# A block of ones at the front of a hybrid decoder layer, earlier raw weights, probabilities scaled on ScalarE, and accumulators split as they are finished

## The chip, the cores and the metric

The kernel runs on one core of a Trainium2 chip. The metric is the device time of one execution in microseconds (us). Five engines work side by side, each in the order of its own list of instructions, and wait for each other by semaphores: TensorE (PE, with its weight loads as PEld), VectorE (DVE), ScalarE (ACT), GpSimd (POOL) and SyncE (SP), which here only starts transfers.

## The reference

One layer on x of 2048 tokens by 1024 channels, float32, with 256 memory tokens. The lines that matter here:

```python
h = rms_norm(x, norm_g)                       # one combined projection w_in of h
a = rwkv7_mix(...)                            # 8 heads x 64
b = sliding_window_sink_attn(...)             # 8 heads x 64, window 128
kv = rms_norm(mem, mem_norm_g) @ w_mem_kv     # memory_cross_attn: keys and values of mem
p = softmax(q @ km.T * 128 ** -0.5); c = p @ vm   # 4 heads x 128
...
# each branch * SiLU(gate) is projected to 1024 channels, weighted by sigmoid gates,
# the three are added, and the sum goes through w_out and is added to x
```

## The kernel before, in words

Tokens are worked in four superblocks of 512 (`sb` 0 to 3). Activations stand transposed, channels on partitions. Every large product is in float32 precision by three matmuls: both operands are split in a high part (rounded to the matmul format, by ScalarE) and a low part (the rest, by VectorE), and `gemm3` (L426) issues high by high (L430), low by high and high by low (L431, L432). A weight block goes through `wblock` (L405): a DMA of 128x512 into a `raw` buffer (three of them, L411), the high copy on ScalarE (L412), the subtraction on VectorE (L413), both into a `whl` buffer (eight). In superblock 0 the finished pair is written to DRAM (L416), and superblocks 1 to 3 fetch it from there whole (L408), without ScalarE or VectorE. So superblock 0 has much more work on those two engines than the others.

At the front, `mem` and the first x blocks are loaded (L341, L351) on the SP queue, then the constants, then raw weights. `norm_T` (L435) squares the rows (L446 on ScalarE, L444 on VectorE), scales them (L451), transposes them on TensorE (L456, 128x128 pieces) and copies the transposed columns out of PSUM as high part (L460, ScalarE) and low part (L461, VectorE); for `mem` these columns are the tiles `mB`. `mem_kv` then multiplies them with `w_mem_kv` (L430 to L432 with 256 columns). `onesw`, a block of ones, is made at L476 to L479 and is used later for column sums.

Then superblock 0 weaves two streams: the recurrent branch (`stream_r`; its projections, the token statistics L472 and the products L731 of its inverse, whose operands QE, QO and BK come from a VectorE chain L703 to L719) and the attention branches (`stream_f`: `cross_head` with the probability scaling L961, the window attention with its exponentials L1066, SiLU gates L898/L899, two merges, the gates L1104). At its end comes the third merge, branch a with `merge(0, ...)` (L1119 multiplies, L1120 adds onto the accumulator, a tile `mB`; eight of them, o = 0 to 7). `x_cols` (L1182, L1184, L1185) prepares the next superblock's x. `output` (L1122) splits all eight accumulators (L1126 on ScalarE into a `g` buffer, L1128 on VectorE into an `mB` buffer), multiplies them with `w_out` (L1137 to L1139) and adds x (L1144).

The order in which each engine holds its instructions isn't the program's. `order` (L265 and on) lets a list scheduler, `lay_out`, deal all instructions to the engines while the program is built, by a modelled time for each and, among those ready, by the lowest `rank`. A rank is the program's position, with corrections in `steps` (L133): the writes of `whl` tiles get 1000 less, but not below a floor of 15, and readers of PSUM outside TensorE get 600 less. On the chip, each engine then runs its list strictly in that order.

## Time and profile before

| | |
|---|---|
| runs | 2280.58, 2281.17, 2286.04 us; median 2281.17 |
| profiled execution | 2283.99 us, its span 2282.2 us, mean granted TensorE clock 0.995 |
| TensorE busy | 2241.2 us (98%), 13684 matmuls |
| VectorE, ScalarE, GpSimd busy | 1541.3 us (68%), 916.9 us (40%), 148.6 us (7%) |
| TensorE busy from 600 to 1100 us (superblocks 1 and 2 in part) | 498.16 of 500 us |
| TensorE busy from 300 to 320 us, 560 to 582 us, 582 to 590 us | 14.20 of 20, 20.50 of 22, 3.81 of 8 us |
| VectorE busy in the same three stretches | 18.10, 20.05, 7.25 us |

The profiled execution is the one from which all rows are taken; its time is the span and 1.8 us around it. A row of the waits names the engine and line that waited, the engine, tile and line that it waited for last, the sum of time, the number of times and the longest. A row of the timeline gives the start, the duration, engine, line and operation, the tiles written and read, and in brackets the idle time before it and what ended it. A row of the windows gives, for a stretch of time, the busy time of PE, PEld, DVE, ACT and POOL with the number of instructions, the granted TensorE clock (1.00 is full speed), the share of the DMA engines in use and GB/s. Superblock 0 ends, by its last output product, at 628.5 us.

### The profile page before, as it was taken

To read this page: it belongs to the slowest core of one execution; us is meant where nothing else is said; L and a number is where in the kernel's file an instruction comes from. 1 tells how busy PE (TensorE), PEld (TensorE's weight loads), DVE (VectorE), ACT (ScalarE), POOL (GpSimd) and SP (SyncE) were. 2 spreads that over 40 slices of the span, in tenths; PEclk is the share of its full clock that TensorE was granted. 3 is DMA by queue.
4 is the path that set the end of the run, shared out by engine and by line. 5 is a ranking of instruction groups with operands and counts; after the bars stand their busy time and mean duration, and the time that the engine had idled before them with its cause. 6 is when DMAs were issued, how large, how long until landed. Compare 5 with 4: busy or idle time off the path is not lost.

```text
span 2282.2 us, 36933 instructions
## 1 busy us (share of the span) xinstructions
PE 2241.2 (98%) x13684; PEld 1814.2 (79%) x13684; DVE 1541.3 (68%) x3967; ACT 916.9 (40%) x2006; POOL 148.6 (7%) x209
## 2 busy tenths in 40 slices
PE   7999989999999999999999999999999999999999
PEld 6788778777788877878888877877888887777887
DVE  6799689775568777954427967884345795796312
ACT  5554564545244354433214344442222535434210
POOL 2000010000000010000001001000000001000000
PEclk9999999999999999999999999999999999999999
DMA  6767546679844443437774434445675444343655
GB/s 215 273 225 252 185 153 217 222 258 341 302 155 160 146 148 130 157 138 239 232 265 129 151 127 139 157 136 183 231 252 196 155 147 151 115 153 121 204 193 193
DMA packets 146226, 430.55 MB, mean 189 GB/s; under 512 B 16640, under 2 KB 21120, under 8 KB 146048
## 3 DMA queue, kind: packets, MB, share of 16 engines
q1 hardware_dynamic: 129920, 398.83, 52.1%
q10 hardware_dynamic: 16128, 29.37, 3.9%
q8 instruction: 109, 1.79, 0.3%
q14 instruction: 69, 0.57, 0.1%
HBM read 333.24 MB, written 94.90 MB: 188 GB/s over the span
## 4 chain that ended last, share of the span: by engine, by line
PE 70%; DVE 12%; ACT 3%; DMA 2%; issue 1%; POOL 0%; SPq 0%; ACTq 0%; DVEq 0%; POOLq 0%
PE mm L431 17%; PE mm L430 17%; PE mm L432 16%; PE rw L731 1%; DVE ibc L779 1%; PE mm L1139 1%; PE mm L1137 1%; PE mm L1138 1%; PE rw L852 1%; PE oo L1092 1%; DVE ibc L780 1%; PE oo L967 1%; PE rw L845 1%; DVE Yi L781 1%; PE rw L837 1%
## 5 line engine op out<-in xcount | busy, mean ns | idle before, releaser
L430 PE MATMUL mm<-hH,whl 128*128 128x512 f32 x1888 | 751.1, 398 | 4.6 <-DVE g L899 3.8
L431 PE MATMUL mm<-hL,whl 128*128 128x512 f32 x1888 | 752.4, 398 | 0.0
L432 PE MATMUL mm<-hH,whl 128*128 128x512 f32 x1888 | 747.4, 396 | 0.0
L430 PEld LDWEIGHTS mm<-hH,whl 128*128 128x128 f32 x1888 | 355.7, 188 | 76.7 <-DVE g L899 4.3
L431 PEld LDWEIGHTS mm<-hL,whl 128*128 128x128 f32 x1888 | 355.6, 188 | 71.1 <-issue 0.7
L432 PEld LDWEIGHTS mm<-hH,whl 128*128 128x128 f32 x1888 | 355.8, 188 | 68.6
L412 ACT ACTIVATE whl<-raw 128x512 fp32r<-128x512 f32 x178 | 111.7, 630 | 183.4 <-PE mm L432 79.6
L413 DVE TENSOR_TENSOR whl<-raw,whl 128x512 fp32r<-128x512 f32 x178 | 123.6, 696 | 65.7 <-ACT whl L412 64.6
L430 PE MATMUL mm<-yh,whl 128*128 128x512 f32 x384 | 152.8, 398 | 1.4 <-DVE g L1119 1.4
L431 PE MATMUL mm<-yl,whl 128*128 128x512 f32 x384 | 151.4, 394 | 0.0
L432 PE MATMUL mm<-yh,whl 128*128 128x512 f32 x384 | 151.3, 394 | 0.0
L843 ACT ACTIVATE SP<-Z,Pl 64x64 f32<-64x64 f32 x256 | 88.3, 345 | 118.7 <-DVE Z L853 114.9
L779 DVE STREAM_SHUFFLE ibc<-Nc 128x496 f32<-128x496 f32 (+30 forms) x248 | 113.2, 474 | 0.1
L1119 DVE SCALAR_TENSOR_TENSOR g<-g,mm 128x512 f32<-128x512 f32 x32 | 21.9, 686 | 127.5 <-PE mm L432 127.4
L780 DVE TENSOR_TENSOR ibc<-ibc,Yi 128x496 f32<-128x496 f32 (+30 forms) x248 | 104.7, 422 | 3.5
L781 DVE TENSOR_TENSOR Yi<-Yi,ibc 128x496 f32<-128x496 f32 (+30 forms) x248 | 103.6, 418 | 1.2
L853 DVE SCALAR_TENSOR_TENSOR Z<-rw,Pl,SP 64x64 f32<-64x64 f32 x224 | 63.5, 283 | 46.6 <-PE rw L852 42.9
L1104 ACT ACTIVATE gt<-mm 128x512 f32<-128x512 f32 x64 | 37.8, 591 | 129.3 <-PE mm L432 129.2
L430 PEld LDWEIGHTS mm<-yh,whl 128*128 128x128 f32 x384 | 72.1, 188 | 16.6 <-DVE g L1119 2.5
L432 PEld LDWEIGHTS mm<-yh,whl 128*128 128x128 f32 x384 | 72.1, 188 | 14.8
L1066 ACT ACTIVATE g<-g,mxs,st 128x256 f32<-128x256 f32 (+1 forms) x128 | 74.6, 584 | 22.8 <-DVE mxs L1059 22.5
L431 PEld LDWEIGHTS mm<-yl,whl 128*128 128x128 f32 x384 | 72.2, 188 | 13.9
(1882 smaller groups left out, 3789.6 us busy)
## 6 DMA issues: line engine op xcount, KB each, us to landing
whl<-k SPq DMA_DIRECT2D x486, 512.0 KB, 3.3
k<-whl SPq DMA_DIRECT2D x162, 512.0 KB, 3.2
raw<-in_w_in SPq DMA_DIRECT2D x118, 256.0 KB, 3.7
g<-in_x ACTq DMA_DIRECT2D x32, 256.0 KB, 5.0
out<-g ACTq DMA_DIRECT2D x32, 256.0 KB, 3.6
raw<-in_w_proj SPq DMA_DIRECT2D x24, 256.0 KB, 3.6
rt<-in_x ACTq DMA_DIRECT2D x24, 256.0 KB, 5.2
rt<-in_xt ACTq DMA_DIRECT2D x24, 256.0 KB, 5.5
```

Of the source, the lines that this page charges most:

```text
L412: S.activation(w[:, 0], raw, AF.Copy)
L413: V.tensor_tensor(w[:, 1], raw, w[:, 0].bitcast(F32), op=ALU.subtract)
L430: PE.matmul(out, lh, rh, start=i == 0, stop=False)
L431: PE.matmul(out, lh, rl, start=False, stop=False)
L432: PE.matmul(out, ll, rh, start=False, stop=i == n - 1)
L779: V.stream_shuffle(bc[:, :, :w], N_[:, :, s + 1:], [s] * 32)
L780: V.tensor_tensor(bc[:, :, :w], bc[:, :, :w], Y[:, :, s:s + 1].to_broadcast([128, n, w]), op=ALU.mult)
L781: V.tensor_tensor(Y[:, :, s + 1:], Y[:, :, s + 1:], bc[:, :, :w], op=ALU.add)
L843: S.activation(SP[h, i], Z[h, i, e, c], AF.Copy, scale=g[4][h, c:c + 1])
L853: upds = [V.scalar_tensor_tensor(Sst[h, g[0]] if c == NC_ - 1 else Z[h, i, e, c + 1], pS[h, i, e], g[4][h, c:c + 1], SP[h, i], op0=ALU.mul ...
L1066: S.activation(prs[b][:, i, m0:], prs[b][:, i, m0:], AF.Exp, scale=r2[:, b, i:i + 1], bias=mx[:, b, i:i + 1], accum_out=mx[:, b, 2 + i:3 + i])
L1104: S.activation(t, gp, AF.Tanh, scale=0.5)
```

## The change

Four edits. (1) The block of ones is made at the very front, and WARM = 22 matmuls of it with itself, 128x512, are issued first of all on TensorE, into a PSUM tile (`idle`) that nobody reads. (2) In `steps`, the DMAs into `raw` tiles get the lowered rank too, and its floor becomes FRONT = 30. (3) `cross_head` scales the probabilities in superblock 0 by ScalarE (16 instructions of 128x256); in the other three by VectorE as before. (4) Each accumulator is split right after its own third merge (`split_acc`), instead of all eight at the start of `output`; `x_cols` follows in the program.

```diff
@@ -23,6 +23,8 @@
 SCRATCH = 1024
 FIRST = 1
 RAW = 3
+WARM = 22
+FRONT = WARM + 8
 C = 64
 NC_ = TB // C
 EPS = 1e-6
@@ -151,8 +153,8 @@
             b.after.append(s)
         byname[ins.name] = s
         s.rank = len(out)
-        if any(r[0].startswith("whl") and (s.bytes or r[5] == F32R) for r in s.writes):
-            s.rank = max(s.rank - ahead, min(s.rank, 15))
+        if any(r[0].startswith(("whl", "raw")) and (s.bytes or r[5] == F32R) for r in s.writes):
+            s.rank = max(s.rank - ahead, min(s.rank, FRONT))
         if s.eng != "PE" and any(r[4] for r in s.reads):
             s.rank -= 600
         if s.eng == "DVE" and s.writes and s.writes[0][0].startswith(("ibc", "Yi")):
@@ -334,6 +336,14 @@
         nc.sync.dma_start(t, A[name] if src is None else src)
         return t
 
+    ones1 = cp.tile([128, 1], F32, name="ones1")
+    V.memset(ones1, 1.0)
+    onesw = bp.tile([128, 128], F32R, name="onesw")
+    S.activation(onesw, ones1.to_broadcast([128, 128]), AF.Copy)
+    idle = o_ps().rearrange("p (a b) -> p a b", a=4)
+    for _ in range(WARM):
+        PE.matmul(idle, onesw, onesw.unsqueeze(1).to_broadcast([128, 4, 128]), start=True, stop=True)
+
     mem0 = []
     for i in range(2):
         mem0.append([g2(), g2()])
@@ -473,10 +483,6 @@
 
     ones2 = bp.tile([128, 128], F32R, name="ones2")
     S.activation(ones2.rearrange("p (a b) -> p a b", a=2), bones.unsqueeze(2).to_broadcast([128, 2, 64]), AF.Copy)
-    ones1 = cp.tile([128, 1], F32, name="ones1")
-    V.memset(ones1, 1.0)
-    onesw = bp.tile([128, 128], F32R, name="onesw")
-    S.activation(onesw, ones1.to_broadcast([128, 128]), AF.Copy)
     eye64 = cp.tile([128, 64], F32, name="eye64")
     V.tensor_tensor(eye64, ident[:, :64], ident[:, 64:], op=ALU.add)
 
@@ -898,6 +904,13 @@
         S.activation(t, o, AF.Tanh, scale=0.5)
         V.scalar_tensor_tensor(t, t, 1.0, o, op0=ALU.add, op1=ALU.mult)
         return t
+
+    def scaled_by(t, c, sb):
+
+        if sb:
+            V.tensor_scalar(t, t, c, None, op0=ALU.mult)
+        else:
+            S.activation(t, t, AF.Copy, scale=c)
 
     def split_y(y, yh, yl, br, j, sb):
         a = yp.tile([128, TB], F32R, name="yh")
@@ -958,7 +971,7 @@
             pt = s_ps().rearrange("p (k i t) -> p k i t", k=2, i=2)
             for i in range(2):
                 q = 2 * t2 + i
-                V.tensor_scalar(prs[t2][:, i], prs[t2][:, i], dn[:, q:q + 1], None, op0=ALU.mult)
+                scaled_by(prs[t2][:, i], dn[:, q:q + 1], sb)
                 for kt in range(2):
                     PE.transpose(pt[:, kt, i], prs[t2][:, i, kt * 128:(kt + 1) * 128], ident)
             pts = g2(shape=(128, 2, 256))
@@ -1119,15 +1132,14 @@
                 V.scalar_tensor_tensor(g, g, 1.0, pp, op0=ALU.add, op1=ALU.mult)
                 V.tensor_tensor(accs[o], accs[o], g, op=ALU.add)
 
-    def output(sb, accs):
-        mh, ml = [], []
-        for o in range(8):
-            a = g2(F32R)
-            S.activation(a, accs[o], AF.Copy)
-            b = mp.tile([128, TB], F32R, name="mB")
-            V.tensor_tensor(b, accs[o], a.bitcast(F32), op=ALU.subtract)
-            mh.append(a)
-            ml.append(b)
+    def split_acc(acc):
+        a = g2(F32R)
+        S.activation(a, acc, AF.Copy)
+        b = mp.tile([128, TB], F32R, name="mB")
+        V.tensor_tensor(b, acc, a.bitcast(F32), op=ALU.subtract)
+        return a, b
+
+    def output(sb, mh, ml):
         for n in range(2):
             op = [mm_ps(), s_ps(), mm_ps(), s_ps()]
             for k in range(8):
@@ -1240,11 +1252,14 @@
         if sb + 1 < nsb:
             rope_tables(sb + 1)
             rb = x_scales(sb + 1)
-        for _ in merge(0, *ya, accs, hT, gates=gates):
-            pass
+        parts = []
+        for o in range(8):
+            for _ in merge(0, *ya, accs, hT, gates=gates, orange=(o,)):
+                pass
+            parts.append(split_acc(accs[o]))
         if rb is not None:
             hT = x_cols(sb + 1, rb)
-        output(sb, accs)
+        output(sb, *zip(*parts))
     order(tc, manual)
     es.close()
```

The line numbers of the changed kernel are other ones: L421 to L423 are L411 to L413 of before, L440 to L442 are L430 to L432, L456 and L454 the squares L446 and L444, L461 the scaling L451, L470 and L471 the copies L460 and L461, L466 the transposes L456, L482 is L472, L737 is L731, L904 is L898, L1079 is L1066, L1132 and L1133 are L1119 and L1120, L1139 is L1128, L1194 and L1197 are L1182 and L1185.

Almost all moves lie in superblock 0; the lists of superblocks 1 to 3 hold the same instructions in practically the same order. Three places:

The front, SP's list. Before, it reads from the first x block on (four `rt` and four `g` tiles are x blocks of 128x512; `c_` tiles are constants):

```order
L351 DMA rt<-in_x 128x512 x4
L351 DMA g_108<-in_x 128x512
L351 DMA g_110<-in_x 128x512
L351 DMA g_112<-in_x 128x512
L351 DMA g_114<-in_x 128x512
L334 DMA c_eye_116<-in_eye 128x32
L334 DMA c_bones<-in_bones 128x2
L334 DMA c_ropec<-in_ropec 128x2
L334 DMA c_sinks<-in_sinks 128x8
L1150 DMA g_340<-in_gmask 128x128
L1150 DMA g_343<-in_amask 128x256
L411 DMA raw<-in_w_mk 128x512 x8
```

Now, from the same place:

```order
L361 DMA rt<-in_x 128x512
L421 DMA raw<-in_w_mk 128x512 x3
L361 DMA rt<-in_x 128x512 x3
L361 DMA g_135<-in_x 128x512
L361 DMA g_137<-in_x 128x512
L361 DMA g_139<-in_x 128x512
L361 DMA g_141<-in_x 128x512
L336 DMA c_eye_143<-in_eye 128x32
L336 DMA c_bones<-in_bones 128x2
L336 DMA c_ropec<-in_ropec 128x2
L336 DMA c_sinks<-in_sinks 128x8
```

Three raw blocks of `w_mk` stand behind the first x block and ahead of the other seven.

ScalarE's list at the front, before, from the second square of `mem` on (the numbers keep the buffers apart; `g2_112` and the `rt` are x):

```order
L446 ACTIVATE ibc_187,ss_181<-g2_92 128x512
L446 ACTIVATE ibc_238,ss_236<-rt_100 128x512
L446 ACTIVATE ibc_242,ss_236<-rt_104 128x512
L446 ACTIVATE ibc_289,ss_236<-g2_108 128x512
L460 ACTIVATE mB_173<-rw_198,c_pv_98 128x256
L446 ACTIVATE ibc_293,ss_236<-g2_112 128x512
L460 ACTIVATE mB_174<-as__207,c_pv_98 128x256
L460 ACTIVATE mB_173<-rw_198,c_pv_98 128x256
L460 ACTIVATE mB_175<-rw_216,c_pv_98 128x256
```

and now:

```order
L456 ACTIVATE ibc_261,ss_259<-rt_127 128x512
L422 ACTIVATE whl_372<-raw_373 128x512
L422 ACTIVATE whl_377<-raw_378 128x512
L422 ACTIVATE whl_411<-raw_412 128x512
L456 ACTIVATE ibc_265,ss_259<-rt_131 128x512
L456 ACTIVATE ibc_312,ss_259<-g2_135 128x512
L470 ACTIVATE mB_196<-rw_221,c_pv_125 128x256
L456 ACTIVATE ibc_316,ss_259<-g2_139 128x512
L470 ACTIVATE mB_197<-as__230,c_pv_125 128x256
L470 ACTIVATE mB_196<-rw_221,c_pv_125 128x256
```

The three high copies of raw weights (L422) stand ahead of the second square of x, and the first copy of transposed `mem` (L470) still stands behind the square of the x block `g2_135`, the second behind that of `g2_139`. VectorE's first subtractions (L423) stand, in the same way, around its scaling of `mem` (L461).

The window attention near 300 us, ScalarE's list. Before (`rt<-rk` belongs to the recurrent branch, `g2_3226` to `g2_3242` hold scores, `g2_3482` is a SiLU gate that leaves PSUM):

```order
L412 ACTIVATE whl_3586<-raw_3587 128x512
L693 ACTIVATE rt_3026<-rk__2966,c_pv_98 128x512
L1066 ACTIVATE g2_3226,mxs_3225<-g2_3226,mxs_3225,st8_3217 128x128 x2
L1066 ACTIVATE g2_3227,mxs_3225<-g2_3227,mxs_3225,st8_3217 128x256 x2
L1066 ACTIVATE g2_3242,mxs_3225<-g2_3242,mxs_3225,st8_3217 128x256
L412 ACTIVATE whl_3644<-raw_3645 128x512
L898 ACTIVATE g2_3482<-mm_3443 128x512
L711 ACTIVATE rt_3047<-rt_2986,dv_126 128x512
```

and now (the scores are `g2_3249` and on, the gate is `g2_3505`):

```order
L422 ACTIVATE whl_3573<-raw_3574 128x512
L717 ACTIVATE rt_3070<-rt_3009,dv_153 128x512
L422 ACTIVATE whl_3609<-raw_3610 128x512
L422 ACTIVATE whl_3667<-raw_3668 128x512
L904 ACTIVATE g2_3505<-mm_3466 128x512
L641 ACTIVATE rk__3443<-mm_3404,dv_153 128x512
L1075 ACTIVATE dns_3346<-dns_3346 128x8
L1079 ACTIVATE g2_3249,mxs_3248<-g2_3249,mxs_3248,st8_3240 128x128 x2
L1079 ACTIVATE g2_3250,mxs_3248<-g2_3250,mxs_3248,st8_3240 128x256
```

The gate's copy out of PSUM stood behind five rows of exponentials, and now stands ahead of them. On TensorE at the same place, four projection matmuls stood between the first and the second group of the products L731 (eight of 128x128 in each), and thirteen stand between the groups of L737 now; and from the statistics (L472, now L482), whose result the products' operands are made from, to the first group it was 22 projection matmuls, and now it is 41.

The end of superblock 0, VectorE's list. Before, from the last third merge's addition on (`hL` and `rt` are the next x, an `mB` of L1128 is a split; the numbers keep the buffers apart):

```order
L1120 TENSOR_TENSOR mB_4476<-mB_4476,g2_5913 128x512
L1185 SCALAR_TENSOR_TENSOR hL_6180<-rt_6201,c_pv_98,hH_6179 128x512
L1182 TENSOR_TENSOR rt_6206<-rt_6206,rt_6001 128x512
L1182 TENSOR_TENSOR rt_6211<-rt_6211,rt_6001 128x512
L413 TENSOR_TENSOR whl_6371<-raw_6372,whl_6371 128x512
L1182 TENSOR_TENSOR rt_6216<-rt_6216,rt_6001 128x512
L1185 SCALAR_TENSOR_TENSOR hL_6180<-rt_6206,c_pv_98,hH_6179 128x512
L1185 SCALAR_TENSOR_TENSOR hL_6180<-rt_6211,c_pv_98,hH_6179 128x512
L413 TENSOR_TENSOR whl_6390<-raw_6391,whl_6390 128x512
L1185 SCALAR_TENSOR_TENSOR hL_6180<-rt_6216,c_pv_98,hH_6179 128x512
L1128 TENSOR_TENSOR mB_6227<-mB_2706,g2_6225 128x512
L413 TENSOR_TENSOR whl_6429<-raw_6430,whl_6429 128x512
```

and now, from the last but one:

```order
L1132 SCALAR_TENSOR_TENSOR g2_5895<-g2_5895,mm_6189 128x512
L1139 TENSOR_TENSOR mB_6180<-mB_3977,g2_6178 128x512
L423 TENSOR_TENSOR whl_6394<-raw_6395,whl_6394 128x512
L1132 SCALAR_TENSOR_TENSOR g2_5936<-g2_5936,mm_6215 128x512
L1133 TENSOR_TENSOR mB_4394<-mB_4394,g2_5895 128x512
L1133 TENSOR_TENSOR mB_4499<-mB_4499,g2_5936 128x512
L423 TENSOR_TENSOR whl_6413<-raw_6414,whl_6413 128x512
L1139 TENSOR_TENSOR mB_6206<-mB_4394,g2_6204 128x512
L1194 TENSOR_TENSOR rt_6246<-rt_6246,rt_6024 128x512
L1139 TENSOR_TENSOR mB_6232<-mB_4499,g2_6230 128x512
L1194 TENSOR_TENSOR rt_6251<-rt_6251,rt_6024 128x512
L423 TENSOR_TENSOR whl_6452<-raw_6453,whl_6452 128x512
```

Before, seven of the eight splits stood behind these seven rows of the next x (L1182, L1185); now six splits stand among the merges, and the last two behind the last addition with one row of the next x between them.

## The prediction

> **What bounds the kernel now.** First the page: TensorE is busy for nearly all of the span. Then the windows, cut where superblock 0 ends, to see where the little idle time lies.
>
> ```profile
> span 2282.2 us, 36933 instructions
> PE 2241.2 (98%) x13684; PEld 1814.2 (79%) x13684; DVE 1541.3 (68%) x3967; ACT 916.9 (40%) x2006; POOL 148.6 (7%) x209
> 0.00:628.50 628.50, 598.16 (x3620) 485.45 (x3621) 480.77 (x1168) 321.12 (x676) 49.43 (x74) 0.98 0.70 240
> 628.50:1180.00 551.50, 548.83 (x3362) 443.75 (x3361) 360.80 (x947) 203.38 (x453) 34.09 (x47) 1.00 0.53 174
> ```
>
> TensorE idles 30.3 us in superblock 0 and 2.7 us in the next one (first column less second), and only in superblock 0 is the clock below full. The change acts there alone, so it can win only these idle times and the slow clock. The waits of TensorE say what the idle time waits for.
>
> ```profile
> PE rw L456 <- DVE g L451: 10.3, 1, 10.3
> PE mm L1139 <- DVE mB L1128: 4.2, 1, 4.2
> PE mm L430 <- DVE g L899: 3.8, 1, 3.8
> PE mm L430 <- ACT whl L412: 3.4, 2, 2.6
> PE mm L430 <- DVE g L1119: 1.4, 1, 1.4
> PE rw L731 <- DVE QO L737: 1.1, 1, 1.1
> PE rw L731 <- DVE whl L737: 1.0, 1, 1.0
> PE as__1483 L472 <- ACT g L921: 0.9, 1, 0.9
> PE rw L731 <- DVE QE L737: 0.9, 1, 0.9
> ```
>
> A wait has a second price. Windows of 3.41 us, laid on the places where the clock changes, show it: columns are the window, TensorE's busy time, and, third from the end, the granted clock.
>
> ```profile
> 135.10:138.51 3.41, 2.51 (x20) 1.91 (x18) 3.32 (x6) 1.11 (x2) 0.00 (x0) 1.00 0.78 272
> 138.51:141.92 3.41, 3.41 (x23) 3.19 (x23) 3.31 (x8) 0.51 (x2) 1.58 (x2) 0.50 0.72 250
> 298.94:302.35 3.41, 1.31 (x9) 0.87 (x8) 3.32 (x8) 3.39 (x13) 0.00 (x0) 1.00 0.97 335
> 302.35:305.77 3.42, 1.68 (x4) 1.41 (x5) 3.30 (x8) 2.52 (x8) 1.54 (x1) 0.50 0.69 246
> 305.77:309.18 3.41, 3.41 (x9) 2.67 (x9) 3.36 (x5) 0.00 (x0) 0.43 (x1) 0.50 0.15 53
> 312.60:316.01 3.41, 1.45 (x8) 0.78 (x7) 3.33 (x6) 0.78 (x2) 0.00 (x0) 1.00 0.40 130
> 316.01:319.42 3.41, 3.41 (x19) 2.79 (x19) 2.96 (x8) 0.62 (x2) 0.00 (x0) 0.50 0.67 219
> 582.25:585.66 3.41, 0.29 (x2) 0.00 (x0) 3.41 (x7) 2.61 (x5) 0.00 (x0) 1.00 0.93 344
> 585.66:589.07 3.41, 2.35 (x6) 1.87 (x7) 3.34 (x6) 0.00 (x0) 0.00 (x0) 0.50 0.83 236
> 589.07:592.49 3.42, 3.42 (x10) 2.64 (x9) 2.47 (x5) 0.63 (x1) 0.00 (x0) 0.50 1.02 405
> 581.92 0.39 PE L1137 MATMUL as__6256<-whl,g 128*128 128x512 f32 x1
> 582.15 0.39 PE L1138 MATMUL as__6256<-whl,g 128*128 128x512 f32 x1
> 588.17 0.63 PE L1139 MATMUL as__6256<-whl,mB 128*128 128x512 f32 x1
> 588.59 0.63 PE L1137 MATMUL mm<-whl,g 128*128 128x512 f32 x1
> ```
>
> After a window with little TensorE work the clock is at half, and stays there until a window was full. The last four rows give the price: starts of 128x512 matmuls lie 0.23 us apart at full clock and 0.42 at half, so 45% of the busy time in a half-clock window is lost. Of the slow windows that is 2.3 us after the wait at 300 (5.09 us of work), 1.5 us after 313, 2.6 us after 582 (5.77 us), and 1.5 us after 135.
>
> **The front.** The rows around the first matmuls (PE's first row ends the wait of 10.3 us):
>
> ```profile
> 2.02 0.31 ACT L479 ACTIVATE onesw<-ones 128x128 fp32r<-128x128 f32 x1
> 10.30 0.47 PE L456 MATMUL rw<-c_ident,g 128*128 128x128 f32 x1 [10.30 <-DVE g L451]
> 10.88 0.63 ACT L446 ACTIVATE ibc<-g 128x512 bf16<-128x512 f32 x1 [1.01 <-DMA g<-in_x]
> 12.09 0.47 ACT L460 ACTIVATE mB<-rw,c_pv 128x256 fp32r<-128x256 f32 x1 [0.48 <-PE rw L456]
> 12.13 1.45 SPq L411 DMA_DIRECT2D raw<-in_w_mk  x3
> 15.94 0.62 ACT L412 ACTIVATE whl<-raw 128x512 fp32r<-128x512 f32 x1
> 16.61 0.58 PE L430 MATMUL mm<-mB,whl 128*128 128x256 f32 x1 [2.64 <-ACT whl L412]
> 17.02 0.68 DVE L413 TENSOR_TENSOR whl<-raw,whl 128x512 fp32r<-128x512 f32 x1
> 19.05:22.46 3.41, 3.41 (x18) 3.41 (x18) 2.54 (x7) 0.63 (x1) 0.99 (x2) 1.00 0.66 214
> 22.46:25.87 3.41, 3.41 (x31) 3.41 (x30) 2.61 (x7) 3.04 (x8) 0.00 (x0) 1.00 0.26 85
> ```
>
> The clock column reads 1.00 here, but 18 matmuls fill the one window and 31 (part of them shorter) the next: TensorE ran at half speed until 22.46, when its first full window had ended.
>
> The warm-up: with `onesw` ready at 2.33, 22 matmuls at 0.42 us would end at 11.6. The first window that they fill ends somewhere between 5.8 and 9.2 us; from then on they go at 0.23, so 8 to 16 are slow and the block ends between 9.0 and 10.6. Until 10.30 TensorE idles, which hides it. At worst it pushes the transposes by 1.3 us.
>
> The raw weights: three 256 KB blocks now pass ahead of seven x blocks on SP's queue. At about 330 GB/s (an estimate from the full windows above) that is 2.4 us later for x. This matters, because ScalarE works in order: its first copy of transposed `mem` (12.09) still stands behind the square of an x block that came at 10.88 and now comes near 13.3, so it starts near 14.1, and the second copy waits for one more x block. VectorE's scaling of `mem` gets two to three subtractions of 0.68 us among its four rows, so the transposes start near 11 instead of 10.30. Against that, the first weights are split long before they are needed, so the first real matmul comes near 14.8 instead of 16.61, and the `mem` columns are complete near 19, some 2 us later than now. Before, the 5.9 us from 16.61 to 22.46 were slow and did 3.2 us worth of work. Now most of that can be done by 19 and the rest by 20.5, if the clock is full: a gain of 2. If the clock has fallen back, the same work ends at 22 to 25.5: from 0 to a loss of 3. If x costs nothing, the gain is 4. **I take 1.5 us of gain**, between the first two, and keep -4 to +3.
>
> A sentence on a rule. The Trainium skill ("TensorE: Matmul & The Clock Gate", Part 4: PE-mode transpose) says that transposes don't count as busy for the clock. By that rule the warm block's clock is lost during the 16 transposes that follow it, the front would gain nothing, and the sum would be 2273.1. The trace doesn't contradict it, and doesn't prove it: the clock stayed at half through the transposes at 10.30 to 14, which filled only about half of their windows. This is the first rival below.
>
> **Near 300 us.** The wait of 3.8 us is for a SiLU gate that holds a PSUM buffer:
>
> ```profile
> 301.82 0.60 ACT L898 ACTIVATE g<-mm 128x512 f32<-128x512 f32 x1
> 304.09 0.80 PE L430 MATMUL mm<-hH,whl 128*128 128x512 f32 x1 [3.84 <-DVE g L899]
> ```
>
> ScalarE came to the gate only at 301.82, behind five rows of exponentials. Now the gate stands ahead of them, so this wait goes, with its 2.3 us of half clock. What is late next is the VectorE chain to the operands of L731: before, 22 matmuls (5.1 us) and this loss of 6.1 us gave it 11 us after the statistics, and 41 matmuls at 0.23, 9.4 us, now stand between. I leave a wait of 2 us, too short for the clock. **Gain 4.1** (0 to 6.1).
>
> At 313 the second group of L731 waited 1.1 and 0.9 us for VectorE (its operands multiplied at L736, L737), with four matmuls, 0.9 us, to cover it. Thirteen, 3 us, cover it now. Wait and half clock were 3.5 us; **gain 3** (0 to 3.5).
>
> **The end of superblock 0.** The 4.2 us are for the second split, which VectorE reached at 585.97 after seven rows of the next x. VectorE is full in these windows (3.41 and 3.34 of 3.41), so something must move back: the next x, which is wanted only at 628.5. Splits now follow each merge, 8 of 0.70 us against rows of the next x that leave from the same stretch, so VectorE's load before 582 hardly grows. **Gain 4.2 + 2.6 = 6.8** (2 to 6.8).
>
> **Smaller parts.** The scaling on ScalarE takes 16 rows from VectorE and lays them on an engine with more room.
>
> ```profile
> L961 DVE TENSOR_SCALAR g<-g,dn x16: 340/346/366, 80.5 to 175.1; 128x256 f32<-128x256 f32 x16
> ```
>
> 5.5 us leave VectorE; on ScalarE they should take 7.5 at 0.47 each (the row at 12.09, same shape). No row of the waits worth a microsecond names L961: I count nothing directly. The stall at 135 (0.9 and its 1.5 of clock) stands in the same order as before: nothing (0 to 2.4). Of the 1.4 us (L1119) and the 1.0 (L731 for `whl`), I take 1. Two more table loads on ScalarE, near 550 us, are hidden by its idle time (40% busy).
>
> **New waits.** The order of 600 us is dealt anew, and may have waits of its own; those of before at 300, 313 and 582 make 16.4 us with their clock. I take **4 us of new ones** (0 to 12): two waits of 1 us and one with a half-clock window.
>
> **The sum.** -1.5 - 4.1 - 3 - 6.8 - 1 + 4 = -12.4, from 2283.99 us: **2271.6 us**. The profiled execution lies 2.8 above the median shown, 2281.17, so part of the gap to that median is this choice of base; I don't correct for it.
>
> **Rivals.**
>
> *The clock falls back at the front.* From 11 to 19 us TensorE has 16 transposes (1.8 us at full clock) and matmuls that come as the columns do; a window with a third of work, as at 313 (1.45 of 3.41), closes the clock. Then half speed lasts again until a window is full, near 24. The window at 135 had as much as 2.51, and the clock fell all the same. Against it: the weights now lie ready, so that the 2.64 us of waiting ahead of the first matmul (row at 16.61) don't stand behind the transposes. Front +2 instead of -1.5: 2275. Chance 0.15.
>
> *The new order has its own stalls near 300.* The deal is made on modelled times; those moved a copy ahead of exponentials, and may have put another behind. The 7.1 us near 300 and 313 come back: 2278.7. Chance 0.13.
>
> *The end of superblock 0 is bound by transfers.* The DMA share (last column but one) is 0.83 to 1.02 from 582 to 592, and output blocks of 256 KB must be split before use. If TensorE starts 4.2 us sooner it may run out of weights: at most the 6.8 come back, 2278.4. Against it: at 582.15 it lacked no weights. Chance 0.08.
>
> *Slower: in-order ScalarE.* In superblock 0 ScalarE gets the 16 scalings, earlier weight copies and splits. If evacuations of PSUM stand behind these, TensorE's two projection buffers stay full, as at 300. One such wait costs 3.8 + 2.3 = 6.1 us. Without the 4 us above, the sum is -16.4, so three of them end even at 2286, and four make 2292. It decides from 2 us of wait on, where the clock closes too. Against it: ScalarE has 321 of 628 us of work. Chance 0.07.
>
> *It doesn't do what it says:* the block of ones shares a PSUM buffer or ends late, and holds back the transposes: 1.3 us, within the range.
>
> **Chances and range.** The forecast has 0.57. A change of 0.3%, 6.8 us, is about what a measurement of this kernel can tell from none; faster means below 2274.3, slower above 2288.0. The forecast (own range 2264 to 2276) falls below 2274.3 with 0.9, the first rival with 0.45, the next two with 0.2: 0.51 + 0.07 + 0.04 = 0.62. Slower gets 0.07, no difference 0.31. The range runs from 2260 (all waits gone, no new ones, and a full front) to 2284 (a second stall beside the rivals).
>
> **What would show it.** Right: in the changed profile, the wait of L1139 for a split is gone and the windows at 582 to 592 are at full clock; no half clock near 300 to 320; the window before 20 us holds some 30 matmuls. Wrong: half clock between 11 and 24 us; new rows of 2 us or more among the waits of TensorE before 600 us; or idle time beyond 628 us that differs, since there nothing was to change.

## The result, and the profile after

The changed kernel takes 2266.14 us (median of 6 runs, 2262.86 to 2267.61) against 2282.58 us (6 runs, 2280.58 to 2286.04): a ratio of 0.9924, 95% interval 0.9912 to 0.9937, 0.76% faster. (The ratio of the two medians is 0.9928; for the kernels below, too, the ratio given and that of the medians differ by up to 0.1%, some 2 us, so gaps of that size aren't read as differences.) Its profiled execution took 2265.73 us, 18.3 less than that of before.

The page of the changed kernel, its two stretches as the windows show them, and its waits:

```profile
span 2263.9 us, 36938 instructions
PE 2238.6 (99%) x13706; PEld 1813.1 (80%) x13706; DVE 1535.2 (68%) x3951; ACT 926.3 (41%) x2024; POOL 147.8 (7%) x209
...
0.00:628.50 628.50, 612.91 (x3719) 498.74 (x3720) 482.12 (x1164) 336.80 (x706) 48.68 (x74) 0.99 0.72 248
628.50:1180.00 551.50, 549.72 (x3366) 444.34 (x3365) 361.08 (x949) 204.48 (x454) 34.10 (x47) 1.00 0.53 174
```

```profile
PE mm L440 <- DVE g L905: 3.5, 1, 3.5
...
PE oo L345 <- ACT onesw L342: 2.4, 1, 2.4
PE rw L466 <- DVE mB L471: 1.8, 1, 1.8
```

TensorE's idle time in the first 628.5 us fell from 30.3 to 15.6 us; 7.8 us of that fall is the block of ones itself, which counts as busy and does no work. The wait for a split and the two for L737's QO and QE are gone. The wait for a SiLU gate, 3.8 us before, is still there with 3.5 (L905 is L899 of before, L743 is L737; in each experiment below the line numbers differ by a few).

To place the gain, I added up TensorE's work matmul by matmul at full speed, without the block of ones, and read off for equal work how much earlier the other kernel was there. Where the order differs this is good to about 1 us. The lead at a place is one execution against one other, and single executions differ as well: in one of the kernels below, whose list for TensorE is row for row that of before (the opposite, under "The order and the execution apart"), the profiled span is 2276.9 us, 5.3 less than that of before.

```
us in the trace of before        30    130   145   295   312   325   400   555   577   600   1163  1180  2270
lead of the changed kernel, us   1.5   2.4   3.8   2.3   3.8   7.3   6.9   7.0   9.1   16.7  16.3  17.4  17.6
```

The clock, in the windows of the changed kernel (columns as in the prediction; below, an open clock is one at full speed, a closed one at half):

```profile
11.11:14.52 3.41, 2.55 (x18) 1.79 (x16) 3.27 (x10) 2.41 (x7) 0.20 (x1) 1.00 1.07 366
14.52:17.93 3.41, 1.01 (x6) 0.81 (x6) 2.94 (x9) 2.05 (x7) 2.33 (x5) 1.00 0.73 237
17.93:21.35 3.42, 3.24 (x16) 3.27 (x17) 3.42 (x9) 2.71 (x7) 0.12 (x1) 0.50 0.09 29
297.79:301.20 3.41, 0.63 (x3) 0.54 (x4) 3.32 (x6) 0.56 (x1) 0.00 (x0) 1.00 0.79 244
301.20:304.62 3.42, 3.42 (x12) 2.28 (x12) 2.88 (x7) 1.31 (x5) 0.00 (x0) 0.51 0.59 217
574.00:582.00 8.00, 8.00 (x37) 6.64 (x36) 6.93 (x12) 3.97 (x6) 0.00 (x0) 1.00 1.04 407
```

At the output it never falls, and TensorE has no idle time there. Near 300 one window is slow instead of two, behind 313 none. At the front the clock fell back at 17.93.

The front's rows in the changed kernel:

```profile
2.37 7.78 PE L345 MATMUL oo<-onesw 128*128 128x512 f32 x22 [2.37 <-ACT onesw L342]
10.88 0.33 PE L466 MATMUL rw<-c_ident,g 128*128 128x128 f32 x1 [0.74 <-DVE g L461]
13.21 0.46 ACT L470 ACTIVATE mB<-rw,c_pv 128x256 fp32r<-128x256 f32 x1
13.72 0.50 PE L440 MATMUL mm<-mB,whl 128*128 128x256 f32 x2
18.11 0.45 PE L466 MATMUL rw<-c_ident,rt 128*128 128x128 f32 x1 [1.80 <-DVE mB L471]
```

The block ends at 10.15, within the idle time. Weights no longer hold up the start (first product at 13.72 instead of 16.61), but then TensorE waits for the columns of `mem`, so that in the window up to 17.93 it does 1.01 us of work.

### The profile page after: what moved, and what is told of

The parts are those of the page before. It is cut to its first block, busy times and chain, and to the rows that moved or that the text cites. A ratio compares the mean times of both kernels' runs of the same rounds, so it can differ in the third digit from the quotient of the medians.

```text
span 2263.9 us, 36938 instructions
## 1 busy us (share of the span) xinstructions
PE 2238.6 (99%) x13706; PEld 1813.1 (80%) x13706; DVE 1535.2 (68%) x3951; ACT 926.3 (41%) x2024; POOL 147.8 (7%) x209
## 4 chain that ended last, share of the span: by engine, by line
PE 81%; DVE 13%; ACT 2%; DMA 2%; issue 1%; POOL 0%; SPq 0%; ACTq 0%; DVEq 0%; POOLq 0%
PE mm L441 20%; PE mm L440 20%; PE mm L442 19%; PE rw L737 1%; DVE ibc L785 1%; PE mm L1149 1%; PE mm L1150 1%; PE mm L1151 1%; PE rw L858 1%; PE oo L980 1%; PE rw L851 1%; DVE ibc L786 1%; PE rw L843 1%; PE oo L1105 1%; DVE Yi L787 1%
## 5 line engine op out<-in xcount | busy, mean ns | idle before, releaser
L440 PE MATMUL mm<-hH,whl 128*128 128x512 f32 x1888 | 750.5, 397 | 3.5 <-DVE g L905 3.5
L442 PE MATMUL mm<-hH,whl 128*128 128x512 f32 x1888 | 747.4, 396 | 0.0
L440 PEld LDWEIGHTS mm<-hH,whl 128*128 128x128 f32 x1888 | 355.0, 188 | 75.6 <-DVE g L905 3.9
L442 PEld LDWEIGHTS mm<-hH,whl 128*128 128x128 f32 x1888 | 355.2, 188 | 68.0 <-issue 0.2
L422 ACT ACTIVATE whl<-raw 128x512 fp32r<-128x512 f32 x178 | 111.2, 629 | 143.3 <-PE mm L442 89.1
L423 DVE TENSOR_TENSOR whl<-raw,whl 128x512 fp32r<-128x512 f32 x178 | 124.0, 700 | 48.0 <-ACT whl L422 44.4
L440 PE MATMUL mm<-yh,whl 128*128 128x512 f32 x384 | 152.9, 398 | 0.3 <-DVE g L1132 0.3
L442 PE MATMUL mm<-yh,whl 128*128 128x512 f32 x384 | 151.5, 394 | 0.0
L1132 DVE SCALAR_TENSOR_TENSOR g<-g,mm 128x512 f32<-128x512 f32 x32 | 21.8, 682 | 128.1 <-PE mm L442 128.1
L1079 ACT ACTIVATE g<-g,mxs,st 128x256 f32<-128x256 f32 (+1 forms) x128 | 74.6, 584 | 24.8 <-DVE mxs L1072 23.6
L440 PEld LDWEIGHTS mm<-yh,whl 128*128 128x128 f32 x384 | 72.1, 188 | 15.2 <-DVE g L1132 0.9
L442 PEld LDWEIGHTS mm<-yh,whl 128*128 128x128 f32 x384 | 72.1, 188 | 14.8
```

The lines of the kernel that those rows point to most:

```text
L422: S.activation(w[:, 0], raw, AF.Copy)
L423: V.tensor_tensor(w[:, 1], raw, w[:, 0].bitcast(F32), op=ALU.subtract)
L440: PE.matmul(out, lh, rh, start=i == 0, stop=False)
L442: PE.matmul(out, ll, rh, start=False, stop=i == n - 1)
L1079: S.activation(prs[b][:, i, m0:], prs[b][:, i, m0:], AF.Exp, scale=r2[:, b, i:i + 1], bias=mx[:, b, i:i + 1], accum_out=mx[:, b, 2 + i:3 + i])
```

## The experiments

Two theories. **One: each edit is worth what stands at its own place**, so the gains add. **Two: the edits re-deal the order of superblock 0**, and what that order happens to be is the gain. "To deal" is what the scheduler does when it gives each engine its list, and a "deal" is the set of lists that comes of it. Below, a kernel's ratio is to the kernel before, measured together with it; times that were measured apart are compared only roughly.

### Each edit alone

The early split alone: the hunks on `split_acc`, `output` and the loop over `merge(0, ...)`.

```diff
-    def output(sb, accs):
+    def split_acc(acc):
...
+            for _ in merge(0, *ya, accs, hT, gates=gates, orange=(o,)):
+                pass
+            parts.append(split_acc(accs[o]))
```

> The kernel before with the early split alone. Theory one (each edit is worth what stands at its own place): the 4.2 us wait of the output for a split goes, and with it the two half-clock windows behind it, 6.8 us together; nothing else moves by more than 1 us, so some 2275.5 against 2282.3. Theory two (the re-dealt order is what counts): the waits near 300 and 313 us change too, by several us either way, so that the sum lies 3 us or more from 2275.5.

Measured: 2274.86 us, ratio 0.9967 (0.9955 to 0.9980). The wait for a split is gone, those near 300 stand as they were:

```profile
PE mm L430 <- DVE g L899: 3.8, 1, 3.8
...
PE rw L731 <- DVE QO L737: 1.1, 1, 1.1
```

The lead grows from 2.6 us at 577 to 10.2 at 600. As theory one has it: this edit re-deals little, 24 of TensorE's 13684 rows, none ahead of 568 us. For that very reason the clock near 300 says something else:

```profile
302.80:306.21 3.41, 3.17 (x8) 2.49 (x9) 3.37 (x6) 1.02 (x4) 1.98 (x1) 0.50 0.70 231
313.04:316.45 3.41, 2.54 (x22) 2.08 (x21) 3.31 (x9) 0.12 (x1) 0.00 (x0) 1.00 0.67 229
316.45:319.86 3.41, 3.41 (x23) 3.00 (x22) 3.38 (x10) 2.89 (x7) 0.00 (x0) 1.00 0.02 7
```

With the old order and the old waits of 3.8, 1.1 and 0.9 us, one window near 300 is at half clock where the execution of before had two, and none behind 313 where it had one. What a wait costs in clock thus differs between executions; it isn't all the change's doing where it is saved.

The raw transfers' rank alone (FRONT is 6, the same place without the 24 instructions ahead).

```diff
-        if any(r[0].startswith("whl") and (s.bytes or r[5] == F32R) for r in s.writes):
-            s.rank = max(s.rank - ahead, min(s.rank, 15))
+        if any(r[0].startswith(("whl", "raw")) and (s.bytes or r[5] == F32R) for r in s.writes):
+            s.rank = max(s.rank - ahead, min(s.rank, FRONT))
```

> The kernel before with the lowered rank of raw transfers alone. Theory one: the first matmul with weights comes near 14 us instead of 16.6, but at half clock, gain at the front 0 to 1 us; since raw transfers carry the weights of all of superblock 0, the order there is dealt anew and the waits at 300 and 313 us change as they did in the changed kernel (5 us less): 2276 to 2282. Theory two: the waits near 300 belong to the scaling on ScalarE, then the time is within 1.5 us of before.

Measured: 2277.97 us, ratio 0.9977 (0.9968 to 0.9986). The front gives 1.2 us (lead at 30), and its place fits: of 77 rows of TensorE that stand elsewhere, 70 lie in the first 75 us. But the wait near 300 is still there, and so are those at 313 (1.1 and 0.9 us), so the 5 us that I laid to these transfers aren't theirs; the rest comes at the output, where the split is 3.0 us late instead of 4.2:

```profile
PE mm L431 <- DVE g L900: 3.8, 1, 3.8
PE mm L1140 <- DVE mB L1129: 3.0, 1, 3.0
```

The block of ones alone (L345's loop, with the floor of the ranks shifted by the 24 instructions ahead; TensorE's list is otherwise that of before, row for row).

```diff
+    idle = o_ps().rearrange("p (a b) -> p a b", a=4)
+    for _ in range(WARM):
+        PE.matmul(idle, onesw, onesw.unsqueeze(1).to_broadcast([128, 4, 128]), start=True, stop=True)
```

> The kernel before with the 22 matmuls of ones alone; weights and x come as before. Theory one: the transposes from 10.3 us on run at full clock, but the matmuls still wait for the first weights at 16.6 us, so the clock falls back in that gap: gain 0 to 0.5 us. Rival: the clock holds through the gap, then the matmuls from 16.6 to 22.5 run at full speed, gain 2.5 to 3 us at the front. In both the order behind 30 us is the same as before and the waits at 300 and 582 us stay.

Measured: 2279.83 us, ratio 0.9989 (0.9980 to 0.9997). The lead at 30 us is 0.5: the clock fell back during the wait for the first weights, now 4.2 us long:

```profile
PE mm L1144 <- DVE mB L1133: 4.2, 1, 4.2
PE mm L439 <- ACT whl L421: 4.2, 1, 4.2
```

This kernel also tells what was particular to the profiled execution of before: though its waits near 300 and 582 are the old ones, it leads by 2.1 us more between 555 and 570 (the 1.4 us for L1119 don't occur) and by 1.1 us more at 1163 to 1180. Some 3 us of the 18.3 are therefore that execution, not the change.

The scaling on ScalarE alone.

```diff
-                V.tensor_scalar(prs[t2][:, i], prs[t2][:, i], dn[:, q:q + 1], None, op0=ALU.mult)
+                S.activation(prs[t2][:, i], prs[t2][:, i], AF.Copy, scale=dn[:, q:q + 1]) if not sb else V.tensor_scalar(prs[t2][:, i], prs[t2][:, i], dn[:, q:q + 1], None, op0=ALU.mult)
```

> The kernel before with the probabilities of superblock 0 scaled on ScalarE alone. Theory one: 5.5 us less of VectorE time between 80 and 175 us are worth nothing directly, since TensorE waits for it there only 0.3 us; the stall at 135 us with its half-clock window (2.4 us) may go: 2279.5 to 2282.5. Theory two: VectorE is the engine that ends the waits of TensorE up to 320 us, so the waits at 300 and 313 shrink: 3 to 6 us less.

Measured: 2272.03 us, ratio 0.9954 (0.9942 to 0.9967): the largest of the four, 10 us, from rows for which TensorE hardly waits. Where it comes from is odd:

```profile
PE mm L430 <- DVE g L899: 4.6, 1, 4.6
...
PE mm L1139 <- DVE mB L1128: 1.1, 1, 1.1
```

The lead is -1.8 at 312, 1.4 at 325, 5.2 at 577, and 11.0 at 600: the largest step is at the output, 400 us behind the last scaling, where the split now comes 1.1 us late instead of 4.2 and the clock holds. The wait near 300 even grew, and the two for QO and QE at 313 are gone. Theory one says nothing of this. This edit re-deals far more than the others: 531 of TensorE's rows stand elsewhere, up to 600 us.

### All but one

The changed kernel, each time with one edit taken back. First the early split (`output` splits all eight accumulators again, as before):

```diff
-        parts = []
-        for o in range(8):
-            for _ in merge(0, *ya, accs, hT, gates=gates, orange=(o,)):
-                pass
-            parts.append(split_acc(accs[o]))
+        for _ in merge(0, *ya, accs, hT, gates=gates):
+            pass
```

> The changed kernel with all splits at the start of the output again. Theory one (each edit is worth what stands at its own place): the wait for a split and its half clock come back near 570 us, 7 us more than the changed kernel, so 2273 against 2266. Theory two (the order dealt anew decides): the three other edits already moved VectorE's work before 570 us, and less than 4 us come back.

Measured: 2266.60 us, ratio 0.9937 (0.9923 to 0.9950), not to be told apart from the changed kernel (0.9912 to 0.9937; by the medians 0.5 us slower, by the ratios 3). With the splits back in `output`, the wait for them is 0.9 us and costs no clock:

```profile
PE mm L440 <- DVE g L905: 3.5, 1, 3.5
...
PE mm L1152 <- DVE mB L1141: 0.9, 1, 0.9
```

So theory one fails here: worth 7 us alone, the early split is worth at most some 3 us beside the others, because under their order the splits in `output` come in time but for 0.9 us.

The raw transfers at their old rank:

```diff
-        if any(r[0].startswith(("whl", "raw")) and (s.bytes or r[5] == F32R) for r in s.writes):
-            s.rank = max(s.rank - ahead, min(s.rank, FRONT))
+        if any(r[0].startswith("whl") and (s.bytes or r[5] == F32R) for r in s.writes):
+            s.rank = max(s.rank - ahead, min(s.rank, 39))
```

> The changed kernel with the raw transfers at their old rank. Theory one: the waits near 300 and 313 us come back as before (5 us more), and at the front 1 us: 2272. Rival (the scaling did that): 2266 to 2268, only the front is lost.

Measured: 2268.19 us, ratio 0.9940 (0.9927 to 0.9952). Nearer to the rival; the waits L737 for QO and QE didn't come back.

Without the block of ones:

```diff
-WARM = 22
+WARM = 0
```

> The changed kernel without the 22 matmuls of ones. Theory one: the transposes and first matmuls run at half clock up to some 21 us, as they mostly do in the changed kernel behind 18 us; x and the copies pace them anyway, so it costs at most 1 us: 2266 to 2267. Rival (the warm clock is what wins the front): 2 to 3 us more, 2268.5.

Measured: 2267.35 us, ratio 0.9935 (0.9923 to 0.9948). Its lead at 30 us is 1.6, that of the changed kernel 1.5: **beside the early weights, the block of ones bought nothing that can be measured** (alone, its ratio of 0.9989 lies just clear of 1). All of TensorE's and VectorE's other rows are in the same order in both kernels. Its front:

```profile
10.34:13.75 3.41, 2.35 (x10) 1.85 (x11) 3.38 (x9) 1.95 (x6) 0.00 (x0) 1.00 1.03 360
13.75:17.16 3.41, 3.40 (x16) 3.07 (x14) 2.84 (x9) 2.05 (x6) 2.25 (x4) 1.00 0.79 241
17.16:20.58 3.42, 2.31 (x19) 2.20 (x19) 3.42 (x9) 2.97 (x7) 0.40 (x1) 1.00 0.15 57
```

The work, slow at first, stretches and fills the window up to 17.16; from there the clock is full. With the block, the same work at full speed left holes, and the clock fell from 17.93 to 21.35. These are two executions with their windows at different places, so what is shown is that the block's gain is too small to see here, not that it is zero in each execution.

The scaling on VectorE again:

```diff
-                scaled_by(prs[t2][:, i], dn[:, q:q + 1], sb)
+                V.tensor_scalar(prs[t2][:, i], prs[t2][:, i], dn[:, q:q + 1], None, op0=ALU.mult)
```

> The changed kernel with the scaling of superblock 0 on VectorE again. Theory one: 0 to 2.4 us more, as the stall near 135 us and its half-clock window come back or not: 2266 to 2268.5. Rival (VectorE's 5.5 us carry on to the waits near 300 us): 3 us or more, 2269 and up.

Measured: 2273.72 us, ratio 0.9959 (0.9947 to 0.9972). The rival: 7.6 us more than the changed kernel, though the output has no wait for a split. The waits at 313 are back, with two slow windows from 312 (the clock stands third from the end):

```profile
PE mm L440 <- DVE g L905: 3.9, 1, 3.9
...
PE rw L737 <- DVE QO L743: 1.1, 1, 1.1
312.25:315.66 3.41, 3.25 (x17) 2.83 (x18) 2.90 (x8) 0.39 (x1) 0.00 (x0) 0.50 0.63 235
315.66:319.08 3.42, 3.42 (x10) 2.57 (x9) 3.31 (x10) 1.27 (x4) 0.00 (x0) 0.50 0.00 0
```

The four alone add up to 24 us, the four taken back to 11, the change itself is 16.4. They overlap, and the scaling acts far from its own place.

### The order and the execution apart

The scheduler assumes a cost and an engine for each instruction. So the 16 scalings can be executed by one engine while all orders are dealt as if the other did them; TensorE's list is then row for row that of the kernel whose deal is taken (in the traces, all 13684 rows).

```diff
         s = Step(ins, masks)
+        if ins.name in SCALE:
+            s.eng, s.lat, s.dur, s.busy, s.table = "ACT", 35, 508.48, 520.48, 0
...
     orders = lay_out(tc, steps(list(tc.nc.cur_bb.bb.instructions), manual))
+    swap = [s for s in orders["ACT"] if s.ins.name in SCALE]
+    orders["ACT"] = [s for s in orders["ACT"] if s.ins.name not in SCALE]
+    orders["DVE"] = sorted(orders["DVE"] + swap, key=lambda s: s.start)
```

> The kernel before, with the 16 scalings still executed by VectorE, but every engine's order dealt as if ScalarE did them (so the orders are those of the scaling alone on ScalarE, with these 16 rows set into VectorE's list at their planned time). That kernel took 2272.0 us, 10 less than before. If the order dealt anew is what won, this one takes 2272 to 2275; if it is VectorE's 5.5 us, 2281 to 2284, and the wait of 4.2 us for a split stands again.

Measured: 2275.29 us, ratio 0.9972 (0.9963 to 0.9982).

```profile
PE mm L436 <- DVE g L905: 4.5, 1, 4.5
...
PE mm L1147 <- DVE mB L1136: 1.8, 1, 1.8
```

VectorE did all its old work, and 7.4 of the 10 us came all the same.

The opposite, from the scaling alone:

```diff
+            s.eng, s.lat, s.dur, s.busy, s.table = "DVE", 45, 320.68, 235.68, 0
```

> The opposite: the 16 scalings are executed by ScalarE, but every engine's order is dealt as if VectorE did them, so that TensorE's list is word for word that of before. If the order is what won, 2280 to 2283, with the waits at 300, 313 and 582 us as before; if it is VectorE's time, 2272 to 2275.

Measured: 2281.45 us, ratio 1.0001 (0.9991 to 1.0011).

```profile
PE mm L1147 <- DVE mB L1136: 4.7, 1, 4.7
PE mm L436 <- DVE g L905: 3.8, 1, 3.8
...
PE rw L737 <- DVE QO L743: 1.1, 1, 1.1
```

VectorE had 5.5 us less to do, and the time didn't move: all the old waits stand. **The scaling's gain is the order that it causes to be dealt**; VectorE's relief adds to it only under that order (3.3 us between the 2275.29 of the first of the two and the 2272.03 of the scaling alone, which were measured apart).

How far does the order alone take it? The last experiment of this kind changes no instruction, only an assumed time:

```diff
         s = Step(ins, masks)
+        if ins.name in SCALE:
+            s.dur, s.busy = s.dur + 25, s.busy + 25
```

> The kernel before, instruction for instruction; only the time that the list scheduler assumes for each of the 16 scalings is 25 ns longer (346 ns, as the trace shows, instead of 321). Some 400 of TensorE's and 450 of VectorE's rows of superblock 0 stand elsewhere by that. If the time hangs on how the order falls out, it lies 2 us or more from that of before, on either side (2270 to 2290), with other waits near 300 and 582 us; if the order of superblock 0 is of no great weight, it is within 1.5 us.

Measured: 2274.98 us, ratio 0.9969 (0.9957 to 0.9981). With the scaling's measured time told to the scheduler, the kernel is 6.7 us faster, two fifths of what the four edits bring:

```profile
PE mm L433 <- DVE g L902: 4.1, 1, 4.1
...
PE mm L1144 <- DVE mB L1133: 1.8, 1, 1.8
```

It isn't an order of its own, though. Up to 300 us TensorE's list differs in 230 rows from that of the scaling on ScalarE; from there on the two are the same, row for row, to the end. So this is another way into the same order, with no work moved, and one case of a better assumed time: that better times give better orders isn't shown.

The wait for a split follows the deal. It is 4.2, 4.2 and 4.7 us in three kernels with the old order ahead of it (before, the block alone, the opposite above), 3.0 with the raw transfers' order, 1.1, 1.8 and 1.8 in the three with the scaling's, and 0.9 with both (the changed kernel without the early split).

### The wait that is left

Near 300 us, ScalarE and VectorE of the changed kernel:

```profile
297.75 0.60 ACT L904 ACTIVATE g<-mm 128x512 f32<-128x512 f32 x1
...
299.83 0.69 DVE L905 SCALAR_TENSOR_TENSOR g<-g,mm 128x512 f32<-128x512 f32 x1
...
300.57 0.50 PE L440 MATMUL mm<-hH,whl 128*128 128x512 f32 x1 [3.51 <-DVE g L905]
...
303.31 0.69 ACT L641 ACTIVATE rk__3443<-mm,dv 128x512 f32<-128x512 f32 x1 [4.96 <-DVE rr__3114 L726]
```

TensorE has two PSUM buffers for projections. One holds the gate, read last by VectorE at 299.83. The other holds the value of the recurrent branch, whose copy (303.31) waits until VectorE is done with the key, since key and value share one buffer. The experiment gives them two, for one of the eleven `g` buffers:

```diff
-NG = 11
+NG = 10
...
-        k = shift(kp, B_K + p, pcol("mu_k", p), dcol("omu_k", p), sb, "rk_")
+        k = shift(kp, B_K + p, pcol("mu_k", p), dcol("omu_k", p), sb, "rk_", 2)
...
-        v = shift(vp, B_V + p, pcol("mu_v", p), dcol("omu_v", p), sb, "rk_")
+        v = shift(vp, B_V + p, pcol("mu_v", p), dcol("omu_v", p), sb, "rk_", 2)
```

> The changed kernel with a second buffer for the shifted key and value of the recurrent branch, at the cost of one of the eleven g buffers. Near 300 us a projection waits 3.5 us for PSUM, because the value's PSUM tile can't be emptied until the key's buffer is free (ScalarE's row waits there for VectorE). If that is the cause, this wait goes and its half-clock window too: 5 us less in that stretch, 2261 if nothing else changes. Rival: VectorE's chain to L737 ends at the same time and TensorE waits there instead, or the lost g buffer makes new waits: 2265 to 2268.

Measured: 2265.09 us, ratio 0.9928 (0.9916 to 0.9940). The value now leaves PSUM at 291.63, ahead of the gate, and the 3.5 us are gone; but a new wait closes the clock at 336:

```profile
291.63 0.69 ACT L641 ACTIVATE rk__3443<-mm,dv 128x512 f32<-128x512 f32 x1
296.96 0.58 ACT L904 ACTIVATE g<-mm 128x512 f32<-128x512 f32 x1
```

```profile
332.79:336.20 3.41, 1.73 (x20) 1.53 (x21) 3.33 (x6) 0.83 (x2) 0.00 (x1) 1.00 0.70 232
336.20:339.62 3.42, 3.42 (x10) 2.66 (x9) 3.38 (x7) 0.00 (x0) 1.92 (x2) 0.50 0.68 237
```

The lead over the kernel before is 13.7 us at 325 (7.3 in the changed kernel) and 10.3 at 400 (6.9): half is given back in 75 us. That the wait went with the second buffer fits the shared buffer as its cause. But this edit, too, re-deals 264 of TensorE's rows, from 298 us on, and here the buffer and the deal weren't parted. The whole kernel is 1.0 us below the changed one, with intervals that overlap, so I don't call it faster.

## Why the prediction was right, point by point

The time forecast was 2271.6 with a range of 2260 to 2284; it came out at 2266.14. The gain from the profiled execution was to be 12.4 us and was 18.3, of which some 3 us belong to the execution of before. That the sum came near is in part luck: the place near 300 gave 2.6 us less than forecast, and the 4 us set aside for new waits, hardly needed, made up for it. Of the signs named beforehand for being right, only the one at the output came: near 300 there is still a half-clock window, and the windows around 20 us hold 6 and 16 matmuls, not some 30. Of those for being wrong, the half clock between 11 and 24 us came; the one new wait above 2 us is that for `onesw`, ahead of all work.

- **The end of superblock 0**: forecast 6.8, lead gained between 577 and 600 us 7.6. Right in place, price and clock. The early split alone does it, as forecast. But it isn't the only cause: the kernel without it has most of the gain too, from the order of the other edits.
- **Near 313**: forecast 3, measured 3.5 (312 to 325). The waits went, as forecast; of the half-clock window the early split alone shows that it can stay away with the old waits too, so 1.5 of the 3.5 us may be the execution's. The gain hangs on the scaling (its removal brings the waits back), not on the raw transfers as I then supposed in the experiments.
- **Near 300**: forecast 4.1, measured some 1.5 (295 to 312). This step failed. The exponentials did leave ScalarE's way, as forecast; in their place VectorE's rows ahead of L905 held the same PSUM buffer, and the other buffer was held by the value. The prediction looked for the next late thing at the operands of L737; it was the second reader of the same tile. What it gained is one slow window of two, and even that isn't shown to be the change's, since the early split alone has one there under the old order. The prediction also left a wait of 2 us as "too short for the clock" against its own row at 312.60, where 1.45 us of work, so 2.0 us of waiting, closed it.
- **The front**: forecast 1.5, measured 1.5; added up in the same way, the five experiments whose front is that of before lie between 0.7 us behind it and 1.0 ahead at 30 us, and the six kernels with early weights some 1.1 to 1.7 ahead. The mechanism was half right: weights early, columns of `mem` late, clock fallen back at 17.93, as the first rival had it (its 2 us of loss did not come), and still a gain, since the first products were done before. The block of ones has no part in it that can be seen.
- **The transposes** were not what closed the clock: the window from 11.11 to 14.52 holds little else than 16 transposes, and the clock stayed full behind it. It fell after the window with 1.01 us of work.
- **Scaling**: "I count nothing directly" holds to the letter (ratio 1.0001 with the old order). What was missed is that an edit worth nothing directly may cause the order that is worth 7 us; the prediction put the gain at 313 to the order, but not the order to this edit.
- **New waits**: 4 us were set aside; the only new one above 1 us behind the front is for `Z` (L843, 1.4 us, where before it was 0.5), and from 145 to 295 the lead shrinks by 1.5 us. This term was the largest error of the sum. The 135 us place, forecast 0, gave 1.4 (lead 2.4 at 130, 3.8 at 145): its slow window went, as it did in the early split alone, under the old order.
- **Smaller parts**: of the 1 us taken, the 1.0 us of L731 for `whl` stands as it was, and the 1.4 us for L1119 went in the block of ones alone as well, so it is the execution's.
- **Rivals**: DMA did not bound the output; its share is 1.04 from 574 to 582 with TensorE at 8.00 of 8.00. ScalarE's in-order list made no wait worth naming.

That the order is the cause of the gain is shown for the scaling (order and execution apart, and the assumed time). For the early split alone, the gain at its own place is shown, with hardly a row moved elsewhere. What the raw transfers add beyond the front is argued from the overlap of the gains. Why one order has the split 4.2 us late and another 1.1 wasn't tested and stays open. How much of the difference between times that were measured apart is in the sums of single edits stays open.

## What to carry to other kernels

Where a list scheduler deals the order, an edit is two changes: the work it moves, and the new deal for everything behind it. Part them before giving a reason: execute the edit under the old order, and deal the new order without the edit. Here 25 ns more of assumed cost brought 6.7 us, more than the raw transfers or the block of ones alone. Another kernel may as well lose by such a step, so try it and measure. A matmul block to warm the clock gained nothing to be seen where the work behind it left its windows unfilled; and a wait for PSUM ends with the last reader, on whichever engine, so look at all readers and at the other buffer's too.

## What the runs showed of the hardware

Transposes alone open the clock, which I had not expected. In the kernel with the old order and the scaling on ScalarE, TensorE had nothing but 16 transposes until 16.32. The windows:

```profile
10.34:13.75 3.41, 3.17 (x15) 2.70 (x14) 2.92 (x10) 2.84 (x8) 1.57 (x3) 1.00 0.91 269
13.75:17.16 3.41, 0.71 (x4) 0.50 (x4) 3.41 (x10) 2.73 (x8) 1.35 (x3) 1.00 0.56 191
17.16:20.58 3.42, 3.40 (x16) 3.12 (x15) 3.42 (x9) 1.05 (x3) 0.23 (x1) 0.50 0.51 135
```

and the second matmul behind them, from the timeline:

```profile
16.54 0.28 PE L437 MATMUL mm<-mB,whl 128*128 128x256 f32 x1
```

The first matmuls behind them run at full speed (0.28 us, where before it was 0.41), and the clock falls again after the window with 0.71 us of work. The same transposes did not open it in the profiled execution of before, where they were cut by a window's edge at 12.22 and filled about half of two windows. So where the window's edge falls, which differs from execution to execution, decides over up to half a window's work, 1.7 us, at the front. Near 300 us the same shows: the same waits under the same order closed three windows in the execution of before and one in that of the early split alone. That this makes the spread between executions of one kernel (2278.05 to 2287.14 us for that of before) is likely, not shown. The page of the Trainium skill "TensorE: Matmul & The Clock Gate" (Part 1, What's actually happening) says that the window runs freely; these runs agree. Its statement that transposes don't count (Part 4: PE-mode transpose) is not what these windows show.

ScalarE takes 502 ns for the scaling of 128x256 in place (493 to 518, 16 rows), where VectorE took 346: the move costs ScalarE 8.0 us to save VectorE 5.5.
